# Out-projection of each pair of channel blocks, issued as four parts behind the next four dense tiles

## The chip, the cores and the metric

One core of one Trainium2 chip runs the whole program. The metric is the device time of one execution in microseconds; the time before is the median of three runs. One further execution was profiled, and all rows below are of that one.

## What is computed

Two layers of a causal decoder trunk, for a prompt of 1024 tokens and 8 sample tokens, in float32. Layer 0 mixes tokens by two groups of attention-like heads, layer 1 by a gated convolution of width 31 with a LayerNorm over channels. After each of them stands a ConvFFN, which is what the change touches:

```python
def _conv_ffn(h, hist, w_in, w_dw, b_dw, w_out):
    g, u = jnp.split(h @ w_in, 2, axis=-1)
    ext = jnp.concatenate([hist.astype(g.dtype), g], axis=1)
    gc = _dwconv(ext, w_dw, b_dw)            # causal, per channel, width 3
    out = (jax.nn.gelu(gc, approximate=False) * u).astype(h.dtype) @ w_out
```

d_model is 1024 (KD = 8 tiles of 128 channels), the inner width 2816 (NF = 22 blocks of 128 channels). Its result is added to the residual `x`. A final RMSNorm follows.

## The kernel before

Channels lie on partitions, tokens on the free axis. The tokens are worked in two halves: h = 0 is 512 prompt tokens, h = 1 the other 512 and the 8 sample tokens, 520 in all, which each matmul takes as two pieces of 260. Each float32 operand is split into a high and a low part (`split`, L102: a ScalarE cast gives the high part, a subtraction on VectorE, or on GpSimd for out-weights, the low one), and a product is three matmuls: high by high, high by low, low by high. A dense tile (`dense2`, L1106) is 24 matmuls of 512 columns for h = 0 and 48 of 260 for h = 1.

`mlp(l, h, ...)` (L1221) runs the ConvFFN of layer l for one half. `f_in(f)` (L1236) does one block: the gate's dense tile, its copy `gx`, the three taps on ScalarE and VectorE (L1259, L1261), a Gelu, then the up dense tile, the product `ga` (L1272, and L1274 for the sample tokens), and the split of the product into `ah` and `al`, which have three buffers each. `feed` loads raw weight tiles, two ahead, from SP's queue, and splits them in halves between these steps (`halve`): a tile's load is issued when the second half of an earlier one is split. `f_out` (L1282) multiplies two finished blocks by their out-weights and adds the result to `x` for all eight output tiles: 96 matmuls for h = 1, 48 for h = 0, issued in one run between the blocks 2g and 2g + 1. `f_out_last` does the last pair of the whole program and is not touched.

All PSUM results of dense and out tiles come from `mm2` (L1086): three buffers of two banks. An h = 1 out tile takes one buffer, an h = 0 one holds two output tiles. The means of the norms and the convolution's accumulator share one further bank, `dacc`.

Work that is not TensorE's stands in `side`, a queue of generators: `rms_norm`, `conv` (width 31: 21 taps per channel tile on VectorE, 9 on ScalarE and GpSimd), `norm_ln` and `finish` (final norm). Each yields after a step with a price in units. `tick(w)` (L1196) runs steps worth `rate * w` units, so it sets how the side work is interleaved; `side.drain()` runs what is left. The three engines TensorE, ScalarE and VectorE run in exactly the order in which the program is written (`manual_schedule`), GpSimd and SP in an order of the scheduler's. `WAIT` (L1143) is the price of a step that only gives the engines time before and after a mean.

The order around the change: `project(1)` of layer 0, `mlp(0, 0)`, five blocks of `mlp(0, 1)`, the gating stage `glu` for h = 0 (L1349) with the convolution started beside it, the rest of `mlp(0, 1)`, `project(0)` of the convolution's result, `glu` for h = 1, 18 blocks of `mlp(1, 0)` beside the second convolution, `project(1)`, the rest of `mlp(1, 0)`, `mlp(1, 1)`. A drain of the side queue stands between most of these.

## Time and profile before

| | us |
|---|---|
| median of 3 runs (2805.15 to 2810.11) | 2807.58 |
| profiled execution | 2800.44 |
| its span, first to last instruction | 2798.7 |
| TensorE matmuls busy | 2540.9 (91%) |
| VectorE busy | 1742.4 (62%) |
| ScalarE busy | 1219.8 (44%) |
| GpSimd busy | 703.3 (25%) |
| mean granted TensorE clock, share of 2.4 GHz | 0.957 |

Matmuls overlap each other, so a matmul's own duration is longer than the time until the next starts; a row of many matmuls gives the rate. The clock column of the views is the granted TensorE clock as a share of 2.4 GHz; its other level, 1.2 GHz, is 0.5. An idle time before an instruction is put down to the one whose end released it; "A <- B" reads "A waited for B". Lines are those of the kernel before.

### The profile page before, as it was taken

Reading aid. Unit: us, or ns where it says so; the run is one execution under the profiler, and the core shown is the slowest. Engines: PE = TensorE matmul, PEld = TensorE weight load, DVE = VectorE, ACT = ScalarE, POOL = GpSimd, SP = SyncE. Lnnn points to the kernel's source line nnn. Section 1 sums busy time; section 2 is a strip of 40 time slices with the busy share of each in tenths; the row PEclk is TensorE's granted clock in tenths of the full one; section 3 lists DMA queues with packets and bytes.
Section 4 is the critical chain, followed back from the end, with each engine's and each line's share of the span. In section 5 each row is a group of like instructions: output and inputs, shape, how many; then the busy total and the mean of one; then the engine's idle time right before and its main releaser. Section 6 shows DMA issues by size and latency. Waiting matters only on the chain.

```text
span 2798.7 us, 40518 instructions
## 1 busy us (share of the span) xinstructions
PE 2540.9 (91%) x15819; PEld 2269.9 (81%) x15819; DVE 1742.4 (62%) x3117; ACT 1219.8 (44%) x2129; POOL 703.3 (25%) x718
## 2 busy tenths in 40 slices
PE   8999998989899999799898879999888988899997
PEld 7888887867778887688898878987666877899996
DVE  6777677775564444547778665578885554544444
ACT  5566555543433332444434343544443442333332
POOL 2111254251211111123544120145543001111111
PEclk9999998999999999899898989999999999999999
DMA  6222163244223332232222212332232322323221
GB/s 187 74 69 64 50 170 105 88 129 139 81 85 96 101 97 84 71 91 76 88 66 75 79 58 76 86 98 75 76 91 68 91 68 79 97 85 89 83 84 61
DMA packets 319907, 247.05 MB, mean 88 GB/s; under 512 B 12056, under 2 KB 292040, under 8 KB 319684
## 3 DMA queue, kind: packets, MB, share of 16 engines
q1 hardware_dynamic: 308899, 213.09, 25.9%
q0 software_dynamic: 10816, 31.38, 3.8%
q8 instruction: 124, 2.03, 0.3%
q14 instruction: 68, 0.55, 0.1%
HBM read 226.82 MB, written 18.73 MB: 88 GB/s over the span
## 4 chain that ended last, share of the span: by engine, by line
PE 55%; DVE 20%; ACT 7%; issue 6%; DMA 6%; POOL 2%; SPq 0%; ACTq 0%; DVEq 0%; POOLq 0%
PE mm L1116 16%; PE mm L1113 14%; PE mm L141 8%; PE mm L1297 6%; PE mm L1289 5%; DVE wl L104 5%; DMA wr<-in_w_ffn_in 4%; DVE dacc L1396 4%; DVE ga L1261 2%; ACT wh L103 1%; DVE al L104 1%; DVE ga L1272 1%; ACT ah L103 1%; DVE x L1290 1%; ACT ga L1259 1%
## 5 line engine op out<-in xcount | busy, mean ns | idle before, releaser
L1116 PE MATMUL mm<-xn,wh 128*128 128x260 f32 x3840 | 627.0, 286 | 5.7 <-ACT wh L103 1.8
L104 DVE TENSOR_TENSOR wl<-wr,wh 128x512 fp32r<-128x512 f32 x512 | 371.4, 726 | 412.2 <-ACT wh L103 401.2
L103 ACT CAST wh<-wr 128x512 fp32r<-128x512 f32 x536 | 327.3, 614 | 594.5 <-PE mm L1116 217.6
L1113 PE MATMUL mm<-xn,wh 128*128 128x512 f32 x1792 | 556.7, 392 | 0.7 <-DVE x L1290 0.5
L1116 PEld LDWEIGHTS mm<-xn,wh 128*128 128x128 f32 x3840 | 532.6, 190 | 10.9 <-ACT wh L103 3.7
L1113 PEld LDWEIGHTS mm<-xn,wh 128*128 128x128 f32 x1792 | 337.7, 189 | 73.7 <-DVE x L1290 2.1
L104 POOL TENSOR_TENSOR ol<-wr,oh 128x512 fp32r<-128x512 f32 x176 | 230.0, 1327 | 646.8 <-ACT oh L103 613.4
L1116 PE MATMUL mm<-xn,wl 128*128 128x260 f32 x1920 | 390.0, 285 | 2.3 <-DVE wl L104 2.3
L141 PE MATMUL mm<-xn,wh 128*128 128x260 f32 (+2 forms) x1584 | 386.9, 331 | 0.5 <-ACT qraw L309 0.5
L1113 PE MATMUL mm<-xn,wl 128*128 128x512 f32 x896 | 350.2, 391 | 0.1
L1116 PEld LDWEIGHTS mm<-xn,wl 128*128 128x128 f32 x1920 | 298.6, 190 | 3.1 <-DVE wl L104 3.1
L141 PEld LDWEIGHTS mm<-xn,wh 128*128 128x128 f32 x1584 | 268.7, 193 | 27.9 <-issue 8.3
L141 PE MATMUL mm<-xn,wl 128*128 128x260 f32 (+2 forms) x792 | 259.0, 327 | 0.0
L1396 DVE SCALAR_TENSOR_TENSOR dacc<-U,wdw,dacc 128x512 f32<-128x512 f32 x304 | 229.1, 754 | 7.4
L1297 PE MATMUL mm<-ah,oh 128*128 128x260 f32 x672 | 151.2, 309 | 87.7 <-DVE ga L1274 40.5
L1385 POOL TENSOR_TENSOR dp<-dp,s 128x512 f32<-128x512 f32 x144 | 187.5, 1302 | 129.1 <-ACT s L1384 122.7
L1113 PEld LDWEIGHTS mm<-xn,wl 128*128 128x128 f32 x896 | 169.0, 189 | 36.5 <-DVE wl L104 1.0
L1289 PE MATMUL mm<-ah,oh 128*128 128x512 f32 x352 | 150.0, 426 | 47.1 <-DVE ga L1272 23.8
L1297 PEld LDWEIGHTS mm<-ah,oh 128*128 128x128 f32 x672 | 114.3, 208 | 96.3 <-issue 42.8
L1261 DVE SCALAR_TENSOR_TENSOR ga<-gx,wfd,ga 128x544 f32<-128x544 f32 (+1 forms) x176 | 135.2, 768 | 69.1 <-ACT ga L1259 66.0
L141 PEld LDWEIGHTS mm<-xn,wl 128*128 128x128 f32 x792 | 152.2, 192 | 13.0 <-issue 3.2
L1178 DVE TENSOR_TENSOR x<-x,mm 128x520 f32<-128x520 f32 x176 | 117.8, 692 | 56.7 <-PE mm L1297 53.1
(388 smaller groups left out, 4018.4 us busy)
## 6 DMA issues: line engine op xcount, KB each, us to landing
wr<-in_w_ffn_in SPq DMA_DIRECT2D x176, 512.0 KB
wr<-in_w_ffn_out SPq DMA_DIRECT2D x88, 512.0 KB
wr<-in_w_pw SPq DMA_DIRECT2D x48, 512.0 KB
wr<-in_w_in SPq DMA_DIRECT2D x28, 512.0 KB
wr<-in_w_out SPq DMA_DIRECT2D x16, 512.0 KB
xt<-in_x_prompt SPq DMA_DIRECT2D x8, 512.0 KB
xtd<-xs POOLq DMA_DIRECT2D x8, 512.0 KB, 5.0
cb<-cumd SPq DMA_DIRECT2D x8, 512.0 KB
```

Source lines behind the costliest of these rows:

```text
L103: ACT.copy(h, raw)
L104: (eng or DVE).tensor_tensor(out=l, in0=raw, in1=h.bitcast(F32), op=ALU.subtract)
L141: PE.matmul(ps, a[k], b[:, k, :], start=k == order[0] and j == 0, stop=k == order[-1] and j == 2)
L1113: PE.matmul(ps[:, i], a[k], xt[:, r, k], **f)
L1116: PE.matmul(ps[:, q, 0:260], a[k], xt[:, r, k, q * 260:q * 260 + 260], **f)
L1178: DVE.tensor_tensor(out=ways(x[:, m, sl], h), in0=ways(x[:, m, sl], h), in1=outs(ps, h), op=ALU.add)
L1259: ACT.activation(ga, gx[:, 0:m], AF.Identity, scale=wd[0], bias=bfd[:, l, f:f + 1])
L1261: DVE.scalar_tensor_tensor(out=ga, in0=gx[:, t:t + m], scalar=wd[t], in1=ga, op0=ALU.mult, op1=ALU.add)
L1289: PE.matmul(ps[:, q], o[m + q], a, start=i == 0, stop=i == len(js) - 1)
L1297: PE.matmul(ps[:, q, 0:260], o[m], a[:, q * 260:q * 260 + 260], start=i == 0, stop=i == len(js) - 1)
L1385: POOL.tensor_tensor(out=dps[k], in0=dps[k], in1=q, op=ALU.add)
L1396: ins = DVE.scalar_tensor_tensor(out=o, in0=src, scalar=w, in1=accs[k], op0=ALU.mult, op1=ALU.add)
```

## The change

The out-projection of a pair of blocks is cut into four parts of two output tiles. When block 2g begins, the four parts of the blocks 2g - 2 and 2g - 1 are put on a list, and each of the next four dense tiles (gate and up of 2g, gate and up of 2g + 1) is followed by one of them: `behind()` issues the matmuls at once and returns the sum into `x`, which is issued after the Gelu, or after the splits of the act and the weights. The ticks inside the out-projection are gone, those of `f_in` go from 0.85 to 1.0, and the rates go up: 2.6 to 3.0, 2.2 to 2.4, 3.0 to 3.2. `WAIT` goes from 2 to 4 units. Four blocks instead of five of `mlp(0, 1)` run ahead of the gating stage. The last pair of an mlp is still done at its end, as four parts with ticks of 0.5.

```diff
-    uses = [*columns(w_out0[0]), *ffn(0), *ffn(0, 0, 5), *glus(), *ffn(0, 5), *columns(w_pw2[0]),
+    uses = [*columns(w_out0[0]), *ffn(0), *ffn(0, 0, 4), *glus(), *ffn(0, 4), *columns(w_pw2[0]),
...
-    WAIT = 2.0
+    WAIT = 4.0
...
-    RATE, PROJ, CONV = 2.6, 2.2, 3.0
+    RATE, PROJ, CONV = 3.0, 2.4, 3.2
...
         def f_in(f):
...
             dense2(ps, feed.next(), xt, h)
+            add = behind()
             feed.halve("W")
...
             actf(ga, ga, AF.Gelu)
-            tick(0.85)
+            add()
+            tick()
             ps = mm2()
             dense2(ps, feed.next(), xt, h)
+            add = behind()
             feed.halve("W")
...
             acts[f] = (ah, al, oh, ol)
-            tick(0.85)
+            add()
+            tick()
 
         def f_out(fs):
+
             js = [(acts[f][a], acts[f][b]) for f in fs for a, b in ((2, 0), (2, 1), (3, 0))]
-            if h == 0:
-                for m in range(0, KD, 2):
+
+            def part(m):
+                if h == 0:
                     ps = mm2()
                     for q in range(2):
                         for i, (o, a) in enumerate(js):
                             PE.matmul(ps[:, q], o[m + q], a, start=i == 0, stop=i == len(js) - 1)
-                    DVE.tensor_tensor(out=x[:, m:m + 2, LO], in0=x[:, m:m + 2, LO], in1=ps, op=ALU.add)
-                    tick(0.7)
-            else:
-                for m in range(KD):
-                    ps = mm2()
+                    return lambda: DVE.tensor_tensor(out=x[:, m:m + 2, LO], in0=x[:, m:m + 2, LO],
+                                                     in1=ps, op=ALU.add)
+                pss = [mm2() for _ in range(2)]
+                for r, ps in enumerate(pss):
                     for i, (o, a) in enumerate(js):
                         for q in range(2):
-                            PE.matmul(ps[:, q, 0:260], o[m], a[:, q * 260:q * 260 + 260],
+                            PE.matmul(ps[:, q, 0:260], o[m + r], a[:, q * 260:q * 260 + 260],
                                       start=i == 0, stop=i == len(js) - 1)
-                    add_res(m, h, ps)
-                    if m % 2:
-                        tick(0.7)
+                return lambda: [add_res(m + r, h, ps) for r, ps in enumerate(pss)]
+
+            return [lambda m=m: part(m) for m in range(0, KD, 2)]
+
+        parts = []
+
+        def behind():
+
+            return parts.pop(0)() if parts else lambda: None
...
         for g in range(NF // 2):
+            if g:
+                parts.extend(f_out((2 * g - 2, 2 * g - 1)))
             f_in(2 * g)
             yield
-            if g:
-                f_out((2 * g - 2, 2 * g - 1))
             f_in(2 * g + 1)
             yield
-        (f_out_last if finish else f_out)((NF - 2, NF - 1))
+        if finish:
+            f_out_last((NF - 2, NF - 1))
+        else:
+            for part in f_out((NF - 2, NF - 1)):
+                part()()
+                tick(0.5)
...
     m = mlp(0, 1, B[0])
-    run(m, 5)
+    run(m, 4)
```

What the change does to the order of instructions, at three places. First VectorE in `mlp(0, 1)` beside the convolution, from the weight split ahead of the up tile's product. Before (`wl`, `al`: low parts of weight and act; `ga`: the product; `dacc`: a tap of the convolution; `x<-x,mm`: a sum into the residual):

```order
L104 TENSOR_TENSOR wl<-wr,wh 128x512
L1272 TENSOR_TENSOR ga<-ga,mm_14954 128x520
L1274 TENSOR_TENSOR ga<-ga,mm_14954 128x8
L104 TENSOR_TENSOR al<-ga,ah 128x520
L104 TENSOR_TENSOR wl<-wr,wh 128x512
L1396 SCALAR_TENSOR_TENSOR dacc<-U,wdw,dacc 128x512 x2
L1178 TENSOR_TENSOR x<-x,mm_15031 128x520
L1178 TENSOR_TENSOR x<-x,mm_15045 128x520
L1396 SCALAR_TENSOR_TENSOR dacc<-U,wdw,dacc 128x512 x2
L1178 TENSOR_TENSOR x<-x,mm_15061 128x520
L1178 TENSOR_TENSOR x<-x,mm_15075 128x520
```

And with the change:

```order
L104 TENSOR_TENSOR wl<-wr,wh 128x512
L1275 TENSOR_TENSOR ga<-ga,mm_14951 128x520
L1277 TENSOR_TENSOR ga<-ga,mm_14951 128x8
L104 TENSOR_TENSOR al<-ga,ah 128x520
L104 TENSOR_TENSOR wl<-wr,wh 128x512
L1178 TENSOR_TENSOR x<-x,mm_15000 128x520
L1178 TENSOR_TENSOR x<-x,mm_15001 128x520
L1412 SCALAR_TENSOR_TENSOR dacc<-U,wdw,dacc 128x512 x4
L104 TENSOR_TENSOR wl<-wr,wh 128x512
L1250 COPY gx<-ghist 128x2
L1253 COPY glast<-mm_15064 128x10
```

Two sums stand where eight stood with taps between them, and the other six have gone to the three following dense tiles; the taps come four at a time.

Second, VectorE at the end of the 18 blocks of `mlp(1, 0)` (`U<-U,hy`: the subtraction of the LayerNorm's mean; L146 to L149 Newton steps; `s<-U,pv,hy` the scaling by channel). Before, a stretch two blocks ahead of that end:

```order
L1290 TENSOR_TENSOR x<-x,mm_19967 128x2x512
L1435 TENSOR_TENSOR U<-U,hy 128x520
L1290 TENSOR_TENSOR x<-x,mm_19984 128x2x512
L1435 TENSOR_TENSOR U<-U,hy 128x520 x2
L1290 TENSOR_TENSOR x<-x,mm_20006 128x2x512
L1435 TENSOR_TENSOR U<-U,hy 128x520
```

With the change, from the last sum of the 18 blocks on:

```order
L1296 TENSOR_TENSOR x<-x,mm_20300 128x2x512
L1412 SCALAR_TENSOR_TENSOR dacc<-U,wdw,dacc 128x512 x4
L1412 SCALAR_TENSOR_TENSOR s<-U,wdw,dacc 128x512
L1451 TENSOR_TENSOR U<-U,hy 128x520 x8
L146 SCALAR_TENSOR_TENSOR s<-ha,hy 128x520
L147 TENSOR_TENSOR s<-s,hy 128x520
L148 TENSOR_SCALAR s<-s 128x520
L149 TENSOR_TENSOR hy<-hy,s 128x520
L1469 SCALAR_TENSOR_TENSOR s<-U,pv,hy 128x520 x2
L104 TENSOR_TENSOR xn_20407<-s,xn_20407 128x520 x2
```

The subtractions, the Newton steps and the scaling stood between the sums of the last blocks, and now stand in one piece behind the last of them; `xn_20407` is the input of `project(1)`.

Third, VectorE at the end of `mlp(0, 1)`, with the change (`x<-x,mm` are the last out-projection's sums, `xn_16282` the input of `project(0)`); before, all of `U<-U,hy` and all of `xn` stood ahead of the last of these sums:

```order
L1178 TENSOR_TENSOR x<-x,mm_16201 128x520
L1178 TENSOR_TENSOR x<-x,mm_16202 128x520
L1451 TENSOR_TENSOR U<-U,hy 128x512
L1178 TENSOR_TENSOR x<-x,mm_16233 128x520
L1178 TENSOR_TENSOR x<-x,mm_16234 128x520
L1451 TENSOR_TENSOR U<-U,hy 128x512 x2
L146 SCALAR_TENSOR_TENSOR s<-ha,hy 128x512
L147 TENSOR_TENSOR s<-s,hy 128x512
```

The last two subtractions and all that follows them in the norm have moved behind the last sum of the mlp.

## Rows read from the trace of the kernel before

**Rows 1.** The page, parts 1 and 2: busy time, share of the span and instructions of each engine, and the granted clock of TensorE in 40 slices, in tenths.

```profile
PE 2540.9 (91%) x15819; PEld 2269.9 (81%) x15819; DVE 1742.4 (62%) x3117; ACT 1219.8 (44%) x2129; POOL 703.3 (25%) x718
...
PEclk9999998999999999899898989999999999999999
```

**Rows 2.** Windows by stage, us from the span's start: length, then busy time and number of instructions of PE, PEld, DVE, ACT and POOL, the granted clock, the share of the DMA engines and GB/s. In order: mlp(0, 0); the five blocks of mlp(0, 1); glu for h = 0; the rest of mlp(0, 1); the 18 blocks of mlp(1, 0); the rest of mlp(1, 0); mlp(1, 1) without its last out-projection.

```profile
726.30:1117.20 390.90, 370.88 (x1591) 302.17 (x1589) 192.60 (x265) 145.87 (x245) 68.75 (x71) 0.97 0.31 91
1117.20:1218.50 101.30, 80.23 (x587) 77.56 (x586) 50.30 (x94) 40.44 (x69) 12.17 (x11) 0.90 0.23 65
1218.50:1306.20 87.70, 87.66 (x387) 71.93 (x386) 52.38 (x75) 43.54 (x71) 30.78 (x23) 1.00 0.37 108
1306.20:1701.10 394.90, 341.44 (x2615) 335.83 (x2614) 282.94 (x470) 163.35 (x266) 144.04 (x119) 0.91 0.24 70
...
1845.50:2202.90 357.40, 309.68 (x1257) 246.73 (x1257) 278.78 (x382) 168.25 (x285) 157.87 (x138) 0.93 0.26 79
...
2249.60:2345.80 96.20, 83.42 (x343) 65.47 (x341) 55.84 (x76) 37.62 (x63) 10.89 (x10) 0.95 0.24 72
2345.80:2761.80 416.00, 385.84 (x3131) 381.07 (x3129) 195.22 (x412) 134.31 (x229) 59.43 (x53) 0.98 0.29 85
```

**Rows 3.** Windows of single pairs of blocks, same columns: one of mlp(0, 0), one of mlp(0, 1) beside the convolution, one of mlp(1, 0) beside the convolution, one of mlp(1, 1).

```profile
860.40:893.30 32.90, 32.90 (x146) 27.04 (x145) 15.90 (x22) 11.82 (x20) 5.30 (x6) 1.00 0.33 97
1363.30:1406.70 43.40, 39.34 (x295) 38.87 (x294) 35.40 (x58) 18.81 (x31) 20.35 (x17) 0.88 0.25 74
...
1918.90:1959.10 40.20, 34.99 (x146) 27.99 (x146) 34.62 (x47) 19.50 (x33) 21.61 (x19) 0.96 0.27 79
...
2455.10:2491.20 36.10, 34.92 (x290) 34.71 (x289) 17.35 (x34) 11.80 (x20) 5.17 (x4) 1.00 0.31 89
```

**Rows 4.** The chain of work that ended last, in order of time: start, duration, what. A weight load, and two dense tiles of the second half.

```profile
1421.70 3.83 DMA wr<-in_w_ffn_in
...
1803.36 11.52 PE mm L1116 x96
```

**Rows 5.** Waits of TensorE in the rest of mlp(0, 1): us in total, times, longest.

```profile
PE mm L1297 <- DVE ga L1274: 26.1, 7, 6.3
PE mm L1297 <- DVE x L1178: 23.1, 11, 5.5
```

**Rows 6.** Waits of TensorE in the 18 blocks of mlp(1, 0), same columns.

```profile
PE mm L1289 <- DVE ga L1272: 21.9, 6, 4.5
PE mm L1289 <- DVE x L1290: 13.5, 7, 5.9
```

**Rows 7.** VectorE's instructions by line in the pair 1363.3 to 1406.7 of mlp(0, 1): count, then busy us, mean ns of one, and idle time before them with what ended it.

```profile
L1396 DVE SCALAR_TENSOR_TENSOR dacc<-U,wdw,dacc 128x512 f32<-128x512 f32 x21 | 15.8, 753 | 0.5
L104 DVE TENSOR_TENSOR wl<-wr,wh 128x512 fp32r<-128x512 f32 x8 | 7.5, 934 | 3.4 <-ACT wh L103 3.4
L1178 DVE TENSOR_TENSOR x<-x,mm 128x520 f32<-128x520 f32 x9 | 6.0, 689 | 0.2 <-PE mm L1297 0.2
L1261 DVE SCALAR_TENSOR_TENSOR ga<-gx,wfd,ga 128x544 f32<-128x544 f32 x4 | 3.1, 786 | 2.0 <-ACT ga L1259 1.9
L104 DVE TENSOR_TENSOR al<-ga,ah 128x520 fp32r<-128x520 f32 x2 | 1.4, 701 | 1.5 <-ACT ah L103 1.5
L1272 DVE TENSOR_TENSOR ga<-ga,mm 128x520 f32<-128x520 f32 x2 | 1.4, 686 | 0.0
```

**Rows 8.** Waits of TensorE in mlp(1, 1): us in total, times, longest.

```profile
PE mm L1297 <- DVE x L1178: 7.9, 9, 1.2
PE mm L1297 <- DVE ga L1274: 7.4, 6, 1.5
PE mm L1297 <- DVE U L1486: 6.4, 1, 6.4
```

**Rows 9.** The chain of work around norm_ln(1): start, duration, what. A mean of one piece; the table load, Ln and Exp; one pair of channels from its scaling to the sum that follows it.

```profile
2158.73 1.24 PE mean L1133 x2
...
2170.97 1.28 ACT L91
2172.26 0.74 ACT hy L97
2173.03 0.65 ACT hy L100
...
2186.74 0.68 DVE s L1453
...
2190.70 1.14 DVE x L1290
```

**Rows 10.** GpSimd's timeline at norm_ln(1): start, duration, what; in square brackets the idle time before. The last channel tile of the convolution, its addition to the channel sum, and additions of squares.

```profile
2112.23 1.29 POOL L1399 TENSOR_TENSOR U<-dp,s 128x512 f32<-128x512 f32 x1 [2.77 <-DVE s L1396]
2113.60 1.43 POOL L1429 TENSOR_TENSOR hy<-hy,U 128x520 f32<-128x520 f32 x1
...
2140.13 4.65 POOL L1441 TENSOR_TENSOR ha<-ha,s 128x520 f32<-128x520 f32 x3 [8.60 <-ACT s L1440]
```

**Rows 11.** Waits of TensorE in the rest of mlp(1, 0): us in total, times, longest.

```profile
PE mean L1133 <- DVE ha L1154: 5.0, 1, 5.0
```

**Rows 12.** Waits of TensorE in mlp(0, 0): us in total, times, longest.

```profile
PE mean L1133 <- ACT ha L1134: 7.6, 1, 7.6
PE mm L1289 <- DVE x L1290: 5.4, 1, 5.4
```

## The prediction, made before the changed kernel had run

> **What bounds the kernel now.** The span is 2798.7 us and the profiled execution 2800.44 us, 7.1 us under the median of the three runs, 2807.58 us; the sum below is made on 2800.44 and moved up by 7 at the end. About 0.2%, 5.6 us, is what a measurement of this kernel can tell from no change. I read the page first: TensorE is busy 91% of the span, so the time is TensorE's work, its idle gaps, and what its clock costs after them [rows 1]. Then the stages: the first feed-forward block takes 390.9 us with TensorE busy 370.9 at clock 0.97, while the stages with a convolution beside them lose far more, 394.9 against 341.4 at 0.91 and 357.4 against 309.7 at 0.93 [rows 2]. Then single pairs of channel blocks: 32.9 us for the first half of the tokens where nothing disturbs, but 40.2 beside the convolution; for the second half 43.4 beside the convolution and 36.1 without it [rows 3]. The undisturbed price of a second-half pair is three times 96 matmuls at 11.52 us [rows 4], 34.6 us.
>
> The waits say where the pair loses: in layer 0's second half TensorE waits 26.1 us for L1274 (the product that frees the up tile's PSUM buffer) and 23.1 for L1178 (the out-projection's sum into the residual) [rows 5]; in the first half of layer 1 it is L1272 with 21.9 and L1290 with 13.5 [rows 6]. All stand before out-projection matmuls. The out-projection issues eight tile groups in a row, wants a free buffer every 1.4 us, and VectorE still has the product, the splits and the convolution's taps ahead of the sums.
>
> **The stall in the pairs.** Afterwards no run of eight out tiles is left except at the end of each mlp: a part of 24 (second half) or 12 (first half) matmuls follows each dense tile, and its sum stands behind the Gelu, or behind the act split, when that part has long been done. Is VectorE fast enough? One block of layer 0's second half is 17.3 us of TensorE. VectorE's work in it, from the pair's rows [rows 7]: eight taps of 0.753 are 6.0, four weight splits are 2.8 at 0.69 (an estimate: the row's mean is 0.934, and I take the difference for waiting, since the act split of the same size takes 0.701), four sums of 0.689 are 2.8, two L1261 of 0.786 are 1.6, product, act split and small copies 2.0: 15.2. Before it was 11.5 taps a block. Latency comes on top: the idle times before L1261 and before the act split, 1.9 and 1.5 a pair, 1.7 a block. That is 16.9 of 17.3: TensorE stays the bound, closely. For the first half, by the same count with two wide sums of about 1.2, I get 15.6 of 16.45. In the gating stage taps already stand beside dense tiles at this density, and TensorE was busy 87.66 of 87.70 us [rows 2]. I take 0.5 us a pair left over, ends 0 and 3.
>
> The change adds a wait. Act tiles have three buffers, and the old pair is read until the fourth part, behind the up tile of the odd block, so the odd block's act cast now waits for that part, some 2.2 us later than its product. Queued behind it on ScalarE are the next weight cast and the out-weight casts, on VectorE the act split and the sums; the next gate weights are loaded only after the weight split, and land 3.83 us later [rows 4]. The delay is made up in the even block, where the cast waits for nothing: the chain has about 2 us to spare per pair. SP's loads come in the same order; the odd block's are issued some 2 us later, still a half block ahead of use.
>
> **What PSUM allows.** There are three two-bank buffers. In the second half each dense tile and its two part tiles use all three, so the next dense tile needs the buffer of the dense tile just before. It has the part's 2.9 us for that. That fits if VectorE is not late: the product takes 0.69 [rows 7], the reads of the gate tile about 1 (an estimate). The Trainium skill (Perfetto Trace Analysis, Identifying Performance Opportunities) says that the same gap repeating on the engine that should be saturated can mean too few SBUF or PSUM buffers. By it the bubble would stay, since the buffers do, and the sum would be that of the second rival. The trace agrees only in part: the gap repeats in every pair, but with the same three buffers the wait for L1274 is 3.7 us on average beside the convolution (26.1 over 7) and 1.2 without it (7.4 over 6) [rows 5, 8], so VectorE's lateness sets its size.
>
> **What moves to the ends.** Ticks are rarer: per block 6.0 units of side work instead of 8.06 (rate 2.6), or 6.4 instead of 9.3 (rate 3.0). In the instruction orders the side work no longer finishes inside its cover. Three tails then run with TensorE waiting; their prices come from the steps of the same norms in the trace [rows 9, 10].
>
> Tail 1, before layer 1's out-projection of the convolution: all of norm_ln(1) but the early channel sums. From the end of the last dense tile: last splits, sum and five taps 8.4, two GpSimd adds (1.29 and 1.43) 2.7, mean in two pieces (1.24 each, and two short copies) 3.4, eight subtractions and squares paced by GpSimd's adds (1.55 each, seven, plus 2.0) 12.9, mean 3.4, table load, Ln, Exp and Newton 5.4, four channel pairs of 3.96 each (L1453's start to the sum behind it) 15.8, and the last quarter of the dense tile 1.4: 53.4. TensorE could have been there after 2.8 + 5.8 = 8.6. Exposed: 45 us, ends 33 (each z pair starting behind the one before without its wait, 2.7 instead of 3.96, and adds at 1.29) and 55 (every step a fifth longer).
>
> Tail 2, before project(0): last two subtractions, second mean, Newton and all of z: 5.5 + 1.7 + 5.4 + 15.8 + 1.4 = 29.8, less 5.5 of dense tile: 24 us, ends 18 and 30 by the same bounds.
>
> Tail 3, before the second gating stage: five channels of rms_norm(1), about 2.0 each (scaling, cast and split as in a z pair), half covered by the dense tile: 5 us, ends 2 and 9.
>
> **The sum by stages.**
> - Layer 0, second half without the gating stage: before 101.3 + 394.9 = 496.2 [rows 2]. At full clock 33 groups of 11.52 are 380.2; means and transposes 5. What stays: the history load and its transposes 5, waits in the first two blocks 8, the last out-projection 4 and the leftover 5. Tail 2 is 24. Together 431: saves 65.
> - Tail 3: costs 5.
> - Layer 1, first half, without the out-projection between: before 357.4 + 96.2 = 453.6. Eleven pairs of 32.9 are 361.9; the leftover is 5, tail 1 is 45, the mean's wait [rows 11], the last out-projection and cold matmuls 11. Together 423: saves 31.
> - Layer 1, second half: before 416.0, waits of 7.9 and 7.4 in the pairs go, the 6.4 behind the final norm's tiles mostly stay [rows 8]. 32 groups of 11.52 are 368.6, transposes and tables 6, history load 5, the finish tiles 14: 394, saves 22.
> - Layer 0, first half: the 5.4 wait for L1290 [rows 12] goes, and some 2.5 us of half-speed matmuls behind it. The 7.6 for the mean stays: it stands behind the same dense tile in both orders. Saves 8.
> - The raised WAIT spaces means only; I cost it at nothing, because the first means keep their places and the late ones lie in the tails above. Weight order (four blocks instead of five ahead of the gating stage) moves no work: nothing. If the gating stage did not cover the five taps that it gets more, the upper bound of the leftover holds it.
>
> 65 - 5 + 31 + 22 + 8 = 121. So 2800.4 - 121 = 2679, on the scale of the runs 2687 us.
>
> The clock goes along: in the disturbed pair it is 0.88 on average and 1.00 in the quiet one [rows 3], which I have counted by taking pairs at full clock; the tails let it fall, 1 to 2 us each, inside their ends.
>
> **Rivals.**
> - VectorE becomes the bound beside the convolution. For it: 98% loaded by my sum, splits of 0.934 instead of 0.69 if the difference is port time and not waiting, and the new act wait. Then a pair takes 2.5 us more, 18 pairs, 45 us: 2732. Against it: the chain's spare time, and the gating stage. Chance 0.13.
> - Slower: the three PSUM buffers. Dense tiles wait in every half block for VectorE's reads of the dense tile before, and the gain in the pairs beside the convolution is gone: about 8 pairs of 8.4 and 8 of 7.3, 126 us, while the tails of 74 are still paid: 2813. It decides from a lateness of VectorE at these reads of about 1.3 to 2 us over, four half blocks a pair, 1.7 us each being break-even. For it: L1274 was waited for up to 6.3 us [rows 5]. Against it: 3.5 taps fewer per block. Chance 0.07.
> - The gain is only moved: rarer ticks empty the pairs, and the tails take all of it back, within 5.6 us of no change. That needs tails of 195 us against 74. Chance 0.03. The remaining 0.02 are small gains.
>
> **How the numbers follow.** The forecast, 2687, has 0.75, with 2655 to 2720 as its own range (leftover 0 to 3 a pair, 33 us; tails up to 20 either way; first blocks 10). The range to 2745 takes in most of the first rival, and 2650 the lower ends: about 8 in 10. Faster by over 0.2%: 0.75 + 0.13 + 0.02 = 0.90; same 0.03; slower 0.07.
>
> **What would show it.** Pairs beside the convolution near 35 and 33 us with clock 1.00; waits for L1178 and L1290 of before gone; three gaps where TensorE has only means: about 45, 24 and 5 us, with clock below 1. Wrong, if dense tiles (not out tiles) wait for the ScalarE and VectorE reads of the tile before, if pairs stay above 38 us, or if the tail before layer 1's out-projection is over 60 us.

## The result, and the profile after

The changed kernel takes 2693.2 us, median of four runs (2689.7 to 2699.4); the kernel before took 2806.4 on the same chip (2801.6 to 2810.1). The ratio is 0.960, with a 95% interval of 0.9576 to 0.9624: 4.0% faster. The forecast was 2687 us. The profiled span went from 2798.7 to 2693.3 us, 105.4 less where the sum had 121.

The page, parts 1 and 2: TensorE's busy share went from 91% to 93%; in the clock row the slices of 8 that lay beside the first convolution (20, 22 and 24) [rows 1] are gone, and from slice 13 on the low ones lie at the tails, 8 in slices 25 and 26 (tails 2 and 3) and 6 in slice 32 (tail 1), and in the last slice (8).

```profile
PE 2514.4 (93%) x15819; PEld 2247.7 (83%) x15819; DVE 1735.7 (64%) x3117; ACT 1217.2 (45%) x2127; POOL 707.7 (26%) x718
...
PEclk9999998989989999999999998899999699999998
```

Windows by stage, columns as in [rows 2]. In order: mlp(0, 0); four blocks of mlp(0, 1); glu for h = 0; the rest of mlp(0, 1); tail 2 with project(0); glu for h = 1 (tail 3); 18 blocks of mlp(1, 0); tail 1 with project(1); the rest of mlp(1, 0); mlp(1, 1) without its last out-projection.

```profile
724.30:1106.00 381.70, 367.91 (x1590) 299.42 (x1589) 192.92 (x269) 147.20 (x247) 70.43 (x71) 0.98 0.32 94
1106.00:1187.80 81.80, 67.02 (x491) 64.81 (x489) 46.56 (x84) 36.25 (x62) 9.05 (x9) 0.90 0.23 68
1187.80:1274.90 87.10, 87.10 (x384) 72.13 (x385) 55.45 (x79) 44.30 (x72) 36.20 (x27) 1.00 0.35 103
1274.90:1606.80 331.90, 327.99 (x2709) 325.61 (x2707) 264.62 (x453) 147.98 (x247) 136.72 (x114) 1.00 0.30 88
1606.80:1678.40 71.60, 54.61 (x198) 40.62 (x199) 39.36 (x59) 33.01 (x53) 5.32 (x4) 0.81 0.17 51
1678.40:1788.20 109.80, 103.27 (x779) 98.34 (x778) 66.52 (x99) 52.97 (x92) 22.37 (x26) 0.94 0.28 79
1788.20:2081.90 293.70, 289.66 (x1249) 236.03 (x1249) 255.76 (x348) 147.65 (x253) 144.61 (x128) 0.99 0.32 95
2081.90:2174.50 92.60, 58.29 (x393) 53.51 (x393) 43.64 (x58) 31.29 (x52) 15.59 (x11) 0.74 0.19 57
2174.50:2266.00 91.50, 82.62 (x343) 65.53 (x341) 54.55 (x76) 38.85 (x64) 11.10 (x10) 0.94 0.25 75
2266.00:2657.90 391.90, 381.43 (x3130) 379.88 (x3129) 191.78 (x412) 135.70 (x231) 61.32 (x55) 0.99 0.30 90
```

The two stages beside a convolution ran at clock 0.91 and 0.93 before; now they run at 1.00 and 0.99, with TensorE idle for 4 us each. A part of the loss has moved into the fifth and eighth rows, where TensorE waits for a norm and the clock falls to 0.81 and 0.74.

Single pairs, one each of mlp(0, 1) and mlp(1, 0) beside the convolution and one of mlp(1, 1); they answer to the last three of [rows 3].

```profile
1344.10:1379.00 34.90, 34.90 (x291) 34.78 (x290) 30.27 (x52) 16.69 (x28) 18.09 (x15) 1.00 0.31 92
1903.90:1936.90 33.00, 33.00 (x146) 26.99 (x145) 29.35 (x40) 16.91 (x30) 18.25 (x17) 1.00 0.33 96
2419.00:2453.60 34.60, 34.60 (x290) 34.60 (x289) 17.00 (x34) 11.98 (x20) 5.24 (x4) 1.00 0.31 93
```

Waits of TensorE (us in total, times, longest): the two largest in the rest of mlp(0, 1), against 26.1 and 23.1 of [rows 5]; the two largest in the 18 blocks of mlp(1, 0), against 21.9 and 13.5 of [rows 6]; the two largest in mlp(1, 1), against [rows 8]; then tail 1 and tail 2.

```profile
PE mm L1116 <- DVE gx L1258: 1.8, 2, 1.3
PE mm L1116 <- DVE ga L1277: 0.7, 2, 0.5
...
PE mm L1295 <- ACT oh L103: 3.8, 1, 3.8
PE pcv L1359 <- DVE U L1377: 1.4, 1, 1.4
...
PE hps L1216 <- DMA hr<-in_state_ffn_conv: 3.9, 1, 3.9
PE mm L1116 <- DVE U L1502: 2.6, 1, 2.6
...
PE mean L1133 <- POOL ha L1457: 13.7, 1, 13.7
PE mm L1116 <- ACT xn L103: 10.7, 4, 8.7
PE mean L1133 <- POOL hy L1445: 8.9, 1, 8.9
...
PE mm L1113 <- ACT xn L103: 10.9, 4, 8.8
PE mean L1133 <- POOL ha L1457: 5.6, 1, 5.6
```

In these three stages the out-projection no longer waits for the product or for its own sums. What stands there now is small: dense tiles waiting for VectorE's copies of the gate or for the product (2.5 us together), one cast of out-weights, a load, the final norm's own steps. The large waits are those of the norms in the tails.

### The profile page after: what moved, and what is told of

It reads as the page before. It is cut to its first block, busy times and chain, and to the rows that moved or that the text cites. A ratio compares the mean times of both kernels' runs of the same rounds, so it can differ in the third digit from the quotient of the medians.

```text
span 2693.3 us, 40549 instructions
## 1 busy us (share of the span) xinstructions
PE 2514.4 (93%) x15819; PEld 2247.7 (83%) x15819; DVE 1735.7 (64%) x3117; ACT 1217.2 (45%) x2127; POOL 707.7 (26%) x718
## 4 chain that ended last, share of the span: by engine, by line
PE 70%; DVE 10%; issue 5%; ACT 5%; DMA 3%; POOL 3%; SPq 0%; DVEq 0%; ACTq 0%; POOLq 0%
PE mm L1116 21%; PE mm L1113 20%; PE mm L141 8%; PE mm L1295 8%; PE mm L1302 7%; DVE wl L104 2%; PE tp L504 1%; POOL x L563 1%; DMA wr<-in_w_ffn_in 1%; DVE xn L104 1%; ACT xn L103 1%; DVE s L1170 1%; DMA x<-in_cache_fox_v,idx 1%; DMA x<-in_cache_fox_k,idx 1%; PE sc L478 1%
## 5 line engine op out<-in xcount | busy, mean ns | idle before, releaser
L1116 PE MATMUL mm<-xn,wh 128*128 128x260 f32 x3840 | 639.4, 289 | 25.1 <-ACT xn L103 13.4
L104 DVE TENSOR_TENSOR wl<-wr,wh 128x512 fp32r<-128x512 f32 x512 | 366.0, 716 | 367.8 <-ACT wh L103 367.3
L1113 PE MATMUL mm<-xn,wh 128*128 128x512 f32 x1792 | 564.1, 396 | 12.4 <-ACT xn L103 10.9
L1116 PEld LDWEIGHTS mm<-xn,wh 128*128 128x128 f32 x3840 | 541.5, 193 | 36.9 <-ACT xn L103 17.4
L1113 PEld LDWEIGHTS mm<-xn,wh 128*128 128x128 f32 x1792 | 340.7, 190 | 91.2 <-ACT xn L103 14.6
L103 ACT CAST ah<-ga 128x512 fp32r<-128x512 f32 (+1 forms) x88 | 54.9, 624 | 287.6 <-DVE ga L1277 114.4
L1295 PE MATMUL mm<-ah,oh 128*128 128x512 f32 x352 | 140.2, 398 | 10.1 <-ACT oh L103 8.2
L1295 PE MATMUL mm<-ah,ol 128*128 128x512 f32 x352 | 140.2, 398 | 1.8 <-POOL ol L104 1.8
L1295 PE MATMUL mm<-al,oh 128*128 128x512 f32 x352 | 139.7, 397 | 0.0
```

Source lines behind the costliest of these rows:

```text
L103: ACT.copy(h, raw)
L104: (eng or DVE).tensor_tensor(out=l, in0=raw, in1=h.bitcast(F32), op=ALU.subtract)
L1113: PE.matmul(ps[:, i], a[k], xt[:, r, k], **f)
L1116: PE.matmul(ps[:, q, 0:260], a[k], xt[:, r, k, q * 260:q * 260 + 260], **f)
L1295: PE.matmul(ps[:, q], o[m + q], a, start=i == 0, stop=i == len(js) - 1)
```

## The experiments

A pair below is two blocks, from the first matmul of a gate tile to that two blocks on, in the timeline: the mean of the first six pairs behind the gating stage in mlp(0, 1), of pairs 3 to 6 of mlp(1, 0), and of pairs 3 to 10 of mlp(1, 1). The kernel before ran again beside each group of kernels, with medians of 2799 to 2806 us, and each ratio is to those runs.

| kernel | us | ratio to before, 95% interval | mlp(0, 1) | mlp(1, 0) | mlp(1, 1) |
|---|---|---|---|---|---|
| before | 2799 to 2806 | | 43.3 | 40.5 | 36.9 |
| changed | 2693.2 | 0.960 (0.9576 to 0.9624) | 35.4 | 33.0 | 34.9 |
| e1 run of eight | 2898.5 | 1.034 (1.0312 to 1.0367) | 45.9 | 41.4 | 36.8 |
| e2 parts alone | 2715.9 | 0.9694 (0.9674 to 0.9713) | 38.6 | 37.6 | 34.9 |
| e3 faster ticks | 2668.1 | 0.9524 (0.9499 to 0.9549) | 36.7 | 34.0 | 34.9 |
| e4 sum at once | 2720.3 | 0.9711 (0.9693 to 0.9729) | 35.9 | 33.1 | 34.8 |
| e5 ticks in the run | 2791.9 | 0.9972 (0.9957 to 0.9988) | 40.2 | 34.3 | 36.7 |
| e6 split on GpSimd | 2694.2 | 0.9624 (0.9592 to 0.9656) | 37.8 | 35.0 | 34.9 |
| e7 WAIT 2 | 2662.0 | 0.9501 (0.9474 to 0.9529) | 35.3 | 33.0 | 34.9 |
| e8 middle rates | 2663.9 | 0.9512 (0.9480 to 0.9544) | 35.6 | 33.8 | 34.9 |
| e9 rates by stage | 2654.6 | 0.9499 (0.9465 to 0.9532) | 35.6 | 35.4 | 34.9 |
| e10 five blocks | 2666.6 | 0.9532 (0.9502 to 0.9562) | 35.5 | 33.0 | 34.9 |
| e11 fewer taps, one run | 2666.6 | | 35.5 | 33.2 | 34.9 |

### The run of eight, with everything else changed (e1)

```diff
 # against the changed kernel
-            if g:
-                parts.extend(f_out((2 * g - 2, 2 * g - 1)))
             f_in(2 * g)
             yield
+            if g:
+                f_out((2 * g - 2, 2 * g - 1))      # eight tile groups, no tick inside
             f_in(2 * g + 1)
```

> The changed kernel with the out-projection alone put back as a run of eight tile groups behind the even block's up tile; rates, WAIT, the four blocks ahead of the gating stage and every tick stay as changed, so the three tails (some 46, 26 and 11 us) stay too and no tick stands inside a run. Theory (the stalls come from the run of eight, VectorE being late for its sums): pairs beside the convolution go back to 37 to 40 us in layer 0's second half and 34 to 36 in layer 1's first half, 36 in layer 1's second half: 2745 to 2815 us. Rival (less side work per block made the gain): pairs stay within 1 us of 34.6 and 33.0: 2695 to 2720 us.

It was slower than I had expected of any theory: 3.4% over the kernel before, 45.9 us a pair beside the first convolution. Lighter side work, all of it behind dense tiles, gains nothing without the parts. Where the time goes is seen in the waits of TensorE in the rest of mlp(0, 1), and in VectorE's timeline at one run of eight (start, duration, instruction; in brackets the idle time before).

```profile
PE mm L1298 <- DVE ga L1274: 37.1, 9, 6.1
PE mm L1298 <- DVE x L1178: 25.0, 9, 3.9
```

```profile
1348.22 3.12 DVE L1400 SCALAR_TENSOR_TENSOR dacc<-U,wdw,dacc 128x512 f32<-128x512 f32 x4
1351.25 1.05 DVE L104 TENSOR_TENSOR wl<-wr,wh 128x512 fp32r<-128x512 f32 x1
1352.23 0.68 DVE L1272 TENSOR_TENSOR ga<-ga,mm 128x520 f32<-128x520 f32 x1
...
1355.07 1.54 DVE L1400 SCALAR_TENSOR_TENSOR dacc<-U,wdw,dacc 128x512 f32<-128x512 f32 x2
1356.72 0.75 DVE L1400 SCALAR_TENSOR_TENSOR s<-U,wdw,dacc 128x512 f32<-128x512 f32 x1
1357.50 0.75 DVE L1398 TENSOR_SCALAR dacc<-U,wdw 128x512 f32<-128x512 f32 x1
1358.29 0.75 DVE L1400 SCALAR_TENSOR_TENSOR dacc<-U,wdw,dacc 128x512 f32<-128x512 f32 x1
1358.95 1.90 DVE L1178 TENSOR_TENSOR x<-x,mm 128x520 f32<-128x520 f32 x3
1362.70 0.70 DVE L1178 TENSOR_TENSOR x<-x,mm 128x520 f32<-128x520 f32 x1 [1.85 <-PE mm L1298]
1365.30 0.70 DVE L1178 TENSOR_TENSOR x<-x,mm 128x520 f32<-128x520 f32 x1 [1.90 <-PE mm L1298]
```

TensorE finished the up tile at 1345.3 and two out tiles at 1348.4, and wanted the product's buffer; four taps and a split stand ahead of the product, and five more taps ahead of the first sum. Then the picture turns: late in the run VectorE waits for TensorE.

### The run of eight, with half of the ticks inside it (e5)

```diff
 # against e1
-            tick()                 # behind each dense tile
+            tick(0.5)
...
+                    tick(0.5)      # behind every second out tile of the run
```

> The run of eight again, with the same side work per pair as the changed kernel, but half of it put inside the run (1.5 units behind each dense tile, 1.5 behind every second out tile) instead of all of it behind the dense tiles, where the run of eight took 47 us a pair in layer 0's second half. Theory (what counts is that VectorE's work per stretch of TensorE work is even; the run starves VectorE and the dense tiles crowd it): pairs there fall by 6 to 9 us to 38 to 41, still above the 35 of the parts, since inside the run a sum and taps must come every 1.4 us through three PSUM buffers: 2770 to 2810 us, below the kernel before. Rival (the run itself stalls whatever lies in it): 2850 us or more, as the run without ticks (2898). If evenness is all: 2710 us or less.

It took 2791.9 us, 107 less than e1, for the same instructions in another place, within the theory's range. Beside the convolutions a pair fell from 45.9 to 40.2 and from 41.4 to 34.3; in mlp(1, 1), where no side work is left in the steady pairs, nothing moved (36.8 and 36.7). The windows of the first four pairs behind the gating stage (columns as in [rows 2]) of before, e1, e5 and the changed kernel tell it in one column:

```profile
1318.80:1492.60 173.80, 152.64 (x1162) 150.80 (x1162) 135.26 (x224) 75.95 (x124) 80.65 (x66) 0.90 0.25 74
```

```profile
1292.00:1474.30 182.30, 153.99 (x1160) 152.12 (x1159) 118.00 (x198) 66.30 (x109) 61.14 (x49) 0.89 0.22 65
```

```profile
1283.10:1444.60 161.50, 147.65 (x1160) 145.88 (x1159) 118.33 (x201) 67.20 (x110) 63.69 (x51) 0.95 0.25 73
```

```profile
1274.90:1415.80 140.90, 139.97 (x1161) 139.33 (x1160) 117.32 (x200) 67.65 (x112) 64.29 (x52) 1.00 0.29 87
```

VectorE does the same 117 to 118 us of work in 182, 161 and 141 us. It was never the engine with too much to do (65% busy in e1); it had it at the wrong time. Of the 41.4 us between e1 and the changed kernel 27.4 are TensorE standing idle; the other 14.0 are TensorE busy for longer with the same matmuls, at a granted clock of 0.89 instead of 1.00. In mlp(0, 1) the pair shrinks by 10.5 us from e1 to the changed kernel: 5.7 came back by evenness within the old run, and 4.8 only with the parts. In mlp(1, 0) the split is another, 7.1 and 1.3 of 8.4. In mlp(1, 1), without side work, the parts alone are worth 1.8. A run with its ticks placed in yet another way was not tried, so 4.8 is what the parts give over this one placing.

### The parts alone, and faster ticks (e2, e3)

```diff
-    WAIT = 4.0
-    RATE, PROJ, CONV = 3.0, 2.4, 3.2
+    WAIT = 2.0                                 # e2, and five blocks ahead of glu
+    RATE, PROJ, CONV = 4.03, 2.2, 4.65         # e2: 8.06 and 9.3 units a block, as before
+    RATE, PROJ, CONV = 3.5, 3.2, 3.95          # e3, WAIT and blocks as changed
```

> The parts alone: WAIT, the five blocks ahead of the gating stage and the side work per block are those of the kernel before (8.06 and 9.3 units), so nothing is left for the tails. Theory in its plain form (TensorE is the bound with the parts spread): pairs stay near 35 and 33 us, the 72 us of tails go: 2620 to 2650 us. Rival, VectorE the bound: it has 2.7 taps a block more in layer 0 and 3.9 in layer 1, some 2.0 and 2.9 us on top of the 16.9 and some 17 us a block that I counted; pairs of 38 and 39 us eat the tails' gain: 2680 to 2710 us. Second rival (the three PSUM buffers): dense tiles wait for VectorE in every half block, 2740 us or more.

> The changed kernel with rates of 3.5, 3.2 and 3.95 in place of 3.0, 2.4 and 3.2, just enough that the side work ends inside its cover; all else as changed. Theory: all three tails go, about 80 us, and pairs rise by less than 1 us: 2615 to 2645 us. VectorE the bound (1 us more of taps a block in layer 0, 1.5 in layer 1, in pairs): 18 pairs by 2 to 3 us, 2650 to 2680 us.

Both went the way of the first rival, VectorE the bound. e2 came out 6 us above that rival's range, with its pairs of 38.6 and 37.6 us; e3 within it, though its pairs rose by 1.3 and 1.0 us and not by 2 to 3. In e2 tails 1 and 2 are gone and tail 3 is 5 us; in e3 the three shrank from 45.9, 26.4 and 10.6 to 11, 6 and 6.5 us. The first four pairs again, e2 and then e3:

```profile
1307.20:1464.30 157.10, 142.42 (x1161) 139.86 (x1161) 137.44 (x227) 73.17 (x122) 81.06 (x65) 1.00 0.27 82
```

```profile
1276.10:1423.10 147.00, 142.76 (x1161) 141.13 (x1160) 126.24 (x213) 71.36 (x120) 72.29 (x59) 0.99 0.28 84
```

VectorE is busy for 117.3, 126.2 and 137.4 us (changed, e3, e2) and the four pairs take 140.9, 147.0 and 157.1: 83%, 86% and 87%. From the changed kernel to e2 20.1 us more of work make 16.2 us more of time. Less work than the changed kernel's does not shorten them either: e11, below, has 106.9 us of it and takes 142.1. So the changed rates lie about at the point from which VectorE sets the pair, as the sum had it. In mlp(0, 1) with its tail it hardly matters where the work is done: from the gating stage to the second one, faster ticks moved 403.5 us to 400.0. In mlp(1, 0) with its tail it does: 386.2 to 367.9.

### VectorE made lighter (e11)

```diff
 # against e2, in conv's VectorE taps
+            if t % 2 and 1 + NPOOL < t < 30:
+                return prev[0]
```

> The parts alone (old rates, 2716 us), with ten of every 21 VectorE taps of each convolution channel left out; ticks, order and all else stay. If VectorE's lateness makes the pairs 38 us there: they fall to within 0.5 us of 34.6 in layer 0's second half and to 33 to 34 in layer 1's first, some 18 pairs by 3 to 4 us: 2640 to 2665 us. If it is the ticks' work on ScalarE and GpSimd, or the PSUM buffers whatever VectorE does: pairs stay above 37 and the time above 2700 us.

Beside the convolution the pairs fell from 38.6 to 35.5 and from 37.6 to 33.2, with ticks, ScalarE, GpSimd and PSUM as in e2: it is VectorE's lateness. TensorE's waits for VectorE's reads of a dense tile in mlp(0, 1) were 18.3 us in e2 and are 6.0 here. In mlp(1, 0) the lateness reaches TensorE by way of ScalarE, whose cast of the out-weights stands behind the cast of the product: the waits for the out-weights fell from 13.0 to 3.7 us. The first four pairs:

```profile
1306.20:1448.30 142.10, 140.41 (x1161) 139.37 (x1160) 106.89 (x180) 73.36 (x122) 81.56 (x64) 1.00 0.28 86
```

The total, 2666.6 in one run, missed the expectation by 2 us: the pairs beside norm_ln stayed slow (40 and 47 us in mlp(0, 1), 43 and 40 in mlp(1, 0)). The norm has no taps to leave out; that it is its chain that holds up the pairs there is my reading, and no run shows it.

### One split moved to GpSimd (e6)

```diff
 # against e3: one of four low weight halves of a block
-            feed.halve("W")
+            feed.halve("W", POOL)
             actf(ga, ga, AF.Gelu)
```

> The faster rates (3.5, 3.2, 3.95), and one of the four low weight halves of each channel block subtracted on GpSimd instead of VectorE. VectorE loses 0.7 us a block. Theory (with the faster rates VectorE's lateness sets the pair: 36.3 us instead of 35.3 in layer 0's second half, 34 to 37 instead of 33 in layer 1's first): pairs fall by 0.7 to 1.4 us, some 20 pairs: 2640 to 2658 us against 2668. Rival (GpSimd is now late with its adds of the convolution and its out-weight halves, or both engines slow each other): 2668 us or more.

It lost 26 us against e3, as the rival had it. VectorE's lines beside the convolution, first e3 (1276 to 1568 us), then e6 (1278 to 1570): count, busy us, mean ns of one, idle time before.

```profile
L1412 DVE SCALAR_TENSOR_TENSOR dacc<-U,wdw,dacc 128x512 f32<-128x512 f32 x112 | 84.5, 755 | 3.2
L104 DVE TENSOR_TENSOR wl<-wr,wh 128x512 fp32r<-128x512 f32 x65 | 50.8, 782 | 18.7 <-ACT wh L103 17.2 <-PE mm L1302 1.3
L1262 DVE SCALAR_TENSOR_TENSOR ga<-gx,wfd,ga 128x544 f32<-128x544 f32 x32 | 25.1, 785 | 16.1 <-ACT ga L1260 15.6
L104 DVE TENSOR_TENSOR al<-ga,ah 128x520 fp32r<-128x520 f32 x15 | 11.8, 788 | 12.6 <-ACT ah L103 12.6
```

```profile
L1412 DVE SCALAR_TENSOR_TENSOR dacc<-U,wdw,dacc 128x512 f32<-128x512 f32 x112 | 84.4, 754 | 3.2
L104 DVE TENSOR_TENSOR wl<-wr,wh 128x512 fp32r<-128x512 f32 x48 | 40.3, 839 | 13.0 <-ACT wh L103 13.0
L1262 DVE SCALAR_TENSOR_TENSOR ga<-gx,wfd,ga 128x544 f32<-128x544 f32 x32 | 39.7, 1240 | 16.1 <-ACT ga L1260 15.6
L104 DVE TENSOR_TENSOR al<-ga,ah 128x520 fp32r<-128x520 f32 x15 | 17.2, 1148 | 12.6 <-ACT ah L103 12.6
```

VectorE saved 10.5 us of splits and paid 14.6 on the gate's taps (785 to 1240 ns on average; one of the two of each block kept its 785, the other took 1695) and 5.4 on the act splits: the instructions that stand beside GpSimd's new one, and that read two operands from SBUF, were drawn out. The convolution's taps, whose second operand is in PSUM, kept their 754 ns. The Trainium skill (SBUF — State Buffer, Who interferes with whom) states just that: a VectorE instruction with two SBUF inputs contends with a GpSimd instruction that reads SBUF, one with at most one SBUF input, outside VectorE's two-port modes, does not; this trace agrees.

### The place of the sum (e4)

```diff
-            add = behind()
+            behind()()             # the sum at once, ahead of the tile's own reads
...
-            add()
```

> The changed kernel with each part's sum issued right behind the part's matmuls, ahead of the dense tile's own reads on VectorE. Theory (the order on VectorE matters, since a sum that waits for its part holds up the taps and the product behind it, and those free the dense tile's PSUM buffer): VectorE stands 2 to 3 us a half block in the second halves, dense tiles wait 1 to 2 us each there, pairs of 38 to 42 us: 2750 to 2850 us. Rival (only the spreading matters, the place of the sum does not): 2690 to 2700 us, as the changed kernel.

Slower by 27 us, but not for the reason given: the pairs took at most 0.5 us more. The theory falls there; VectorE could afford to stand for the parts (29.5 us in 39 waits in mlp(0, 1)). Of the 25.5 us between the two spans 9.6 lie in the last blocks of mlp(1, 0) and 8 in the rest of mlp(0, 1) with its tail; mlp(0, 0) took 7.8 more, but began 5.6 earlier, behind a stretch that the edit does not touch. In those last blocks VectorE stands 32.8 us for the parts, and TensorE then waits longer for the norm's sums (6.6 instead of 2.8 us) and for ScalarE's out-weight cast and gate copy (8.5 instead of 4.7). The rival, that the place does not matter, falls by the total.

### WAIT, the five blocks, and better rates (e7, e10, e8, e9)

```diff
-    WAIT = 4.0
+    WAIT = 2.0                                 # e7, e8, e9, e10
+    run(m, 5)                                  # e10, and the weights in that order
+    RATE, PROJ, CONV = 3.2, 3.0, 3.7           # e8
+    RATE, PROJ, CONV = 3.2, 3.0, 3.9           # e9, and RATE ahead of mlp(1, 0)'s last blocks
```

> The changed kernel with WAIT back at 2.0. I had costed the raised WAIT at nothing. What is left for the tails shrinks: before layer 0's projection from nine steps to seven, before the second gating stage from five channels of the norm to one, before layer 1's projection by two of the eight channel sums and the end of the convolution. If WAIT only spaces steps (it costs nothing): within 3 us of the changed kernel, 0.960 of before. If its units push work into the tails: tail 3 gives back 6 us, tail 2 some 4 to 8, tail 1 some 3: 12 to 18 us less, 0.954 to 0.956 of before. If means that come too early make TensorE wait in place of it: no gain, and waits for the mean's sum of squares longer than 5 us.

> The changed kernel with WAIT 2.0 and five instead of four channel blocks ahead of the gating stage, to be held against the same with four (2662, 0.950 of before). If the number of blocks moves no work (as I had costed it): within 4 us. If the side work left over counts: three squares of the norm more are left before layer 0's projection, 1.6 us each, one channel more before the second gating stage and one less before layer 1's: 5 to 9 us slower, 2667 to 2671.

> The changed kernel with rates of 3.2, 3.0 and 3.7 (changed: 3.0, 2.4, 3.2; the faster one 3.5, 3.2, 3.95) and WAIT 2.0: what is left for the tails is one channel pair of the norm before layer 0's projection and three before layer 1's, nothing before the second gating stage. Theory (pairs are free up to a rate at which VectorE comes late, and the tails cost the rest): pairs within 0.7 us of the changed kernel's and tails of 6, 0 and 16 us: 2635 to 2660 us, the best so far. Rival (every unit more in a pair costs as much as in a tail): 2668 to 2690 us.

> The changed kernel with WAIT 2.0, rates of 3.2, 3.0 and 3.9, and the rate set back to 3.2 ahead of the last four blocks of layer 1's first half (at 3.7 they took 96.8 us, at 3.2 with WAIT 2.0 they took 87.6). Nothing is left for any tail but one channel pair before layer 0's projection. By stages: layer 1's first 18 blocks and tail 309 to 313 us (327 with the low rate), the last four 88, the rest as with 3.2: 2635 to 2652 us, 0.942 to 0.948 of before, and faster than any so far. Rival (VectorE comes late at 3.9 and the tail's gain goes): 2658 to 2670 us.

WAIT alone is worth 1% (0.9501 against 0.960, intervals apart). By the spans, 30.9 us: 7.1 from the rest of mlp(0, 1) to the end of project(0), 6.9 in the second gating stage, 4.5 in the 18 blocks and project(1), as expected of the tails; and 8.8 that I had not expected, so that the whole came out above the 12 to 18 us forecast. The 8.8 lie in the last blocks of mlp(1, 0), where the norm for mlp(1, 1), by its units, now ends with the seventh of the eight ticks instead of the last one, just ahead of the last out-projection. The five blocks differ from four by 4.5 us in the medians, within the intervals: not settled. The middle rates left tails 2, 3 and 1 at 7.8, 4.2 and 17.4 us, where the theory had 6, 0 and 16, but took 9.2 us more than e7 in mlp(1, 0)'s last blocks and ended 4 us above the theory's range. In those blocks the mean is now asked for before its sum is ready:

```profile
PE mean L1133 <- DVE ha L1154: 7.8, 1, 7.8
```

e9 takes that back (87.7 instead of 96.8 us there), but its pairs in mlp(1, 0) rise to 35.4, and the 18 blocks with their tail took 320.6 us where I had 309 to 313. So VectorE comes late there, as the rival said, though the gain of the tail goes only in part. At 2654.6 e9 has the lowest median, 3 us above its expected range and below the rival's, and cannot be told from e7, e8 and e3 by the intervals. All four beat the changed kernel.

## Why the prediction was right, point by point

- **The pairs, the bulk of the gain.** Forecast 34.6 and 32.9 us with 0.5 left over; measured 35.4, 33.0 and 34.9. VectorE's 15.2 us a block were 30.27 us in the pair above, 15.1, and 117.3 over four pairs, 14.7. That agreement is partly luck, since two errors cancel. The weight splits take longer than the 0.69 us set down (0.875 on average in that pair), and there are 17 taps and not 16, so that the instructions of the pair last 33.0 us together, 16.5 a block; but neighbours on VectorE overlap a little, and they keep it busy for only 30.8 (30.27 of it inside the window). That it would stay the shorter, closely, is what e2, e3 and e11 show: 5.0 us of VectorE work more in a pair (e2) cost 4.1 us.
- **The weight splits, read wrongly.** I took the difference between their mean of 0.934 us [rows 7] and 0.69 for waiting; it is work drawn out beside GpSimd, as the last section shows from the same trace. So the first rival's condition was true in part (0.875 us in the changed pair above, 0.783 over four pairs), and its price of 2.5 us a pair did not come.
- **The cause, in part.** I had put the stall down to the run of eight, whose sums come behind product, splits and taps. e1 and e5 show two things: the run itself, and VectorE's work crowded beside the dense tiles while it is idle in the run. They are of about the same size in mlp(0, 1) (4.8 and 5.7 us a pair); in mlp(1, 0) the crowding is nearly all (7.1 of 8.4).
- **PSUM.** The repeating wait for the up tile's buffer left with the same three buffers. By the rule cited from the Trainium skill (Perfetto Trace Analysis, Identifying Performance Opportunities) it would have stayed; the rule's "can" is right, and the trace disagrees with it as a cause here. Dense tiles wait for VectorE's reads for 2.5 us in all in the rest of mlp(0, 1). The rival came into sight only with VectorE later: 7.4 us in e3 and 18.3 in e2. No run had another number of buffers.
- **The new act wait.** ScalarE waited for the part twice in the rest of mlp(0, 1), 8.8 us together, and TensorE for none of it; in mlp(0, 0) it waited 4.4 us in each of nine pairs, which still took 33.0 us. Nothing, as costed.
- **Tails 1 and 2** were forecast at 45 and 24 us; measured 92.6 - 46.7 = 45.9 and 71.6 - 45.2 = 26.4. The split into steps held too: 8.9, 13.7 and 8.7 us are the waits for the channel sum, the squares and the first channels of z.
- **Tail 3** was mis-sized: 5 forecast, 109.8 - 99.2 = 10.6 measured. The channels came some 2.07 us apart and the first dense tile of the stage was paced by them, over 18 us with the clock at 0.50 to 0.57 for most of it, so that "half covered by the dense tile" was the wrong half of the estimate.
- **The first blocks of mlp(0, 1)** were mis-sized: 81.8 us for four blocks that need 57.6, so 24 over, where I had 13 (5 for the history, 8 for waits). The mean's wait of 5.1 us, which [rows 11] show elsewhere, was not counted here, nor the matmuls at a lower clock (0.90 over the stage).
- **Layer 1's first half** saved 22.5 us instead of 31, with tail 1 as forecast: its last out-projection waited 4.0 us for a ScalarE cast of the out-weights and then ran at a lower clock (0.82 over 14 us), which the 11 us set down for the mean, that out-projection and cold matmuls did not hold. The second pair of the 18 blocks took 40.5 us, with a wait of 3.8 for the same cast, more than the 0.5 a pair left over.
- **The step that failed: "The raised WAIT spaces means only; I cost it at nothing."** Its units take the place of work in the ticks, and so it pushed steps into all three tails and into the last blocks of mlp(1, 0); it cost 28 us by the ratios (e7). The tails were priced rightly because I took their contents from the order as it is; I put them down to the rates alone.
- **By parts of the change**: the parts alone gain 3.1% (e2); the lower rates on top of them 1.6% (e10 against e2); four blocks 0.3%, not settled; WAIT loses 1.0%. Without the parts, the rest of the change loses 3.4% with all ticks behind dense tiles (e1) and is level with before, within 0.3%, with half of them in the run (e5).

The sum of 121 was 15.6 too much, from tail 3 (5.6), the first blocks (11) and layer 1's first half (8.5), less some 9.5 that the other stages and the start gave more than forecast.

## What to carry to other kernels

When one engine waits for another that is only 65 to 80% busy, as here, look at where each one's work lies within the period before looking at totals or buffers: e5 moved nothing but the place of half the side work and took back 107 us. Raise the side work until the periods begin to grow and no further (here VectorE cost nothing at 83% of the period and some time at 86 and 87%), and then look at what is left over for the serial ends, since every unit of spacing that is charged to the same account is work moved there. Before moving work to GpSimd, see which of VectorE's instructions beside it read two operands from SBUF.

## What was not expected of the hardware

GpSimd's subtraction of 1.4 us a block beside VectorE drew VectorE's two-operand instructions from 785 to 1240 ns on average and cost more than it took off (e6). The same goes on in the kernel before, where I had read it as waiting. In the pair of [rows 7], three of the eight weight splits on VectorE, and two instructions on GpSimd (start, duration):

```profile
1367.69 1.80 DVE L104 TENSOR_TENSOR wl<-wr,wh 128x512 fp32r<-128x512 f32 x1
1372.70 0.69 DVE L104 TENSOR_TENSOR wl<-wr,wh 128x512 fp32r<-128x512 f32 x1
1390.58 1.29 DVE L104 TENSOR_TENSOR wl<-wr,wh 128x512 fp32r<-128x512 f32 x1
...
1367.66 1.28 POOL L1429 TENSOR_TENSOR hy<-hy,U 128x512 f32<-128x512 f32 x1
1390.07 1.26 POOL L1385 TENSOR_TENSOR dp<-dp,s 128x512 f32<-128x512 f32 x1 [4.88 <-ACT s L1384]
```

Five of the eight took 0.69 us; the three that ran beside an addition on GpSimd took 0.94, 1.29 and 1.80, and together they make the mean of 0.934. In the whole rest of mlp(0, 1) the splits that ran with nothing on GpSimd took 687 ns, and those that shared over 0.3 us with a GpSimd instruction 1071 ns on average, up to 1803. The convolution's taps, with one operand in PSUM, took 752 and 754 ns in the same two cases, and the sums into `x`, with one operand in PSUM too, 691 and 690.
